# The last two row tiles of a transformer block's output: final products in two column halves, with a hand-written order on two engines

## Chip, cores, metric

One Trainium2 chip, one of its cores. The metric is the device time of the whole kernel in microseconds, the median of several runs. The engines are TensorE (PE, with its weight loads PEld), VectorE (DVE), ScalarE (ACT), GpSimd (POOL) and SyncE (SP, which issues the DMAs). Each works through its own queue in order, and waits for the others on semaphores.

## What is computed

A block of a hybrid encoder: a mixer (pooling and gated linear attention), then a squared-ReLU MLP, then a last RMS norm. The change touches only the end, the second product of the MLP, its residual sum and the last norm:

```python
def rmsnorm(x, g):
    y = xf * lax.rsqrt(jnp.mean(xf * xf, axis=-1, keepdims=True) + EPS)
    return (y * g.astype(jnp.float32)).astype(x.dtype)

def squared_relu_mlp(u, w_ff1, w_ff2):
    hdn = jnp.square(jax.nn.relu(jnp.einsum('bld,df->blf', u, w_ff1)))
    return jnp.einsum('blf,fd->bld', hdn, w_ff2)

# in reference():
        h = h + squared_relu_mlp(rmsnorm(h, norm_ffn[l]), w_ff1[l], w_ff2[l])
    return rmsnorm(h, norm_final)[:, N_META:]
```

The hidden state has 1024 rows (tokens) and 1024 columns, the MLP 4096 hidden channels.

## The kernel before

All products are made of three matmuls each (`mm3`, lines 246 to 248), since both operands are split into a high and a low part. The split of an operand costs one instruction on ACT (L264) and one on DVE (L265).

The second product of the MLP (`ff2`) is a Strassen scheme: seven products `m` = 0 to 6 in place of eight, each of 512 rows by 512 columns over 2048 hidden channels, taken in 16 steps `i` (`NPAIR`). A product works on four row tiles `t` = 0 to 3 of 128 rows, with one PSUM bank of 512 columns for each tile. The table `FF2` says to which quarters of the result `c` each product is added or subtracted; `add` does this on DVE, straight out of PSUM (L1630, L1632). The last product, `m` = 6, goes to one quarter alone: the first 512 columns of row tiles 0 to 3. Rows 4 to 7 are finished earlier.

In that last product the last three steps are held back (`late`). So the four row tiles end one after another instead of all at once: nine matmuls for tile 0, nine for tile 1, nine for tile 2, nine for tile 3. The banks of these four tiles are named b_x, b_x, b_mm and b_ms. Behind each tile its finish follows (`finish_row` with `tail`):

- the addition of the bank to `c` (DVE, L1630);
- the sum of squares of the first 512 columns (ACT Square with its readout, L1605). That of the other 512 columns was made earlier by `top`, which also multiplied these columns by the norm's weight;
- the root: Ln and Exp on ACT (L210, L212), and on DVE the mean (L211) and a Newton step in three instructions (L214, L218, L219);
- the scaling: the right 512 columns on ACT (L1608), the left 512 on DVE (L1609);
- two stores of 256 KB, right and left, both issued by SP (L1611).

Only TensorE's order is written by hand (`manual_schedule` around everything). On ACT, DVE and SP a scheduler sets the order in which the recorded instructions stand.

Of the kernel before, what the change touches and what calls it, by code (L numbers as in the profile page):

```python
# [11 lines left out]
ACT = mybir.ActivationFunctionType  # L12
ALU = mybir.AluOpType
AX = mybir.AxisListType

P = 128
D = 1024
# [3 lines left out]
HALF = 512  # L21
# [4 lines left out]
EPS = 1e-6  # L26
# [4 lines left out]
NPAIR = DFF // P // 2  # L31
# [74 lines left out]
def kernel(  # L106
# [3 lines left out]
    nc = tc.nc  # L110
    x = x[0]
    out = out[0]
# [4 lines left out]
    act, dve, pool, pe = nc.scalar, nc.vector, nc.gpsimd, nc.tensor  # L117
# [20 lines left out]
    def bank(tag):  # L138
        if tag in rota:
            turn_of[tag] = turn_of.get(tag, -1) + 1  # L140
            tag = rota[tag][turn_of[tag] % len(rota[tag])]
        return psp[tag].tile([P, 512], F32, name=f"b_{tag}", tag=tag)
# [20 lines left out]
    gB = left.push("gB", [P, D], F32)  # L163
# [3 lines left out]
    def tiny(n):  # L167
        a = small_at[0]
        small_at[0] += n
        assert small_at[0] <= 128  # L170
        return small[:, a : a + n]

    pscale, bgate, gnorm = tiny(4), tiny(2), tiny(4)
    stat = [tiny(16) for _ in range(4)]
# [22 lines left out]
    def bcast(v):  # L197
        return v[None, :].broadcast_to([P, D])
# [43 lines left out]
    def mm3(ps, n, lhs, rhs, first=True, last=True, more=False):  # L242

        for i in range(n):
            (ah, al), (bh, bl) = lhs(i), rhs(i)
            pe.matmul(ps, ah, bh, start=first and i == 0, stop=False, skip_group_check=more)  # L246
            pe.matmul(ps, ah, bl, start=False, stop=False, skip_group_check=more)  # L247
            pe.matmul(ps, al, bh, start=False, stop=last and i == n - 1, skip_group_check=more)  # L248
# [19 lines left out]
    def ahead(items, n):  # L268

        made = []  # L270
        for x in items:
            made.append(x)
            if len(made) > n:
                yield made.pop(0)
        yield from made
# [125 lines left out]
    S, rings = {}, [W1]  # L401
# [41 lines left out]
    def halves():  # L443
        return [slice(h * HALF, (h + 1) * HALF) for h in range(2)]
# [1138 lines left out]
    def ff2_operands():  # L1583
        for m, i, a in ahead(ff2_raw(), 2):
            q = FF2[m][1]
            w = S["w2"][q[:2]][:, i]
            if len(q) > 2:
                bt = S["bt"][:, i % 2]
                dve.tensor_tensor(bt, w, S["w2"][q[3:]][:, i], ALU.add if q[2] == "+" else ALU.subtract)  # L1589
                w = bt  # L1590
            yield m, i, split(a), split(w)

    def finish_row(t, tail):

        a, (h0, h1) = S["c"][:, t], halves()
        junk = S["w2"]["12"].rearrange("p i c -> p (i c)")[:, (t % 4) * D : (t % 4 + 1) * D]
        if not tail:
            ss = ln_stat[t % 4]
            act.activation(junk, a, ACT.Square, accum_out=ss)
            rs = inv_sqrt(ss, 1, 1.0 / D)  # L1600
            dve.scalar_tensor_tensor(junk, a, rs, gB, ALU.mult, ALU.mult)
            nc.sync.dma_start(out[t * P : (t + 1) * P, :], junk)
            return
        s0, s1 = tails[t]
        act.activation(junk[:, h0], a[:, h0], ACT.Square, accum_out=s0)  # L1605
        dve.tensor_scalar(s1, s1, 1.0 / D, EPS, ALU.mult, ALU.add)
        rs = inv_sqrt(s0, 1, 1.0 / D, s1)
        act.activation(junk[:, h1], a[:, h1], ACT.Copy, scale=rs)  # L1608
        dve.scalar_tensor_tensor(junk[:, h0], a[:, h0], rs, gB[:, h0], ALU.mult, ALU.mult)  # L1609
        for c in (h1, h0):  # L1610
            nc.sync.dma_start(out[t * P : (t + 1) * P, c], junk[:, c])  # L1611

    tails = [(tiny(1), tiny(1)) for _ in range(4)]

    def ff2():
        nc.sync.dma_start(gB, bcast(norm_final))
        h1 = halves()[1]
        b, late, owed = None, [], []

        banks_of = [bank(tag) for tag in ("x", "x", "mm", "ms", "ms", "ms", "ms", "mm")]  # L1620

        def product(t, i, av, bv):
            (ah, al), (bh, bl) = av, bv
            c = slice(t * P, (t + 1) * P)
            mm3(b[t], 1, lambda _: (ah[:, c], al[:, c]), lambda _: (bh, bl), first=i == 0, last=i == NPAIR - 1)

        def add(b, t, r, k, sign):
            a = S["c"][:, 4 * r + t, k * HALF : (k + 1) * HALF]
            if sign > 0:
                dve.tensor_tensor(a, b, a, ALU.add)  # L1630
            else:
                dve.tensor_tensor(a, a, b, ALU.subtract)  # L1632

        def top(t):

            a = S["c"][:, t, h1]
            act.activation(S["w2"]["12"][:, 8 + t], a, ACT.Square, accum_out=tails[t][1])
            dve.tensor_tensor(a, a, gB[:, h1], ALU.mult)

        def leave(m, t):  # L1640

            for at in FF2[m][2]:
                owed.append(lambda b=b[t], at=at: add(b, t, *at))
            if m == 4:
                owed.append(lambda: finish_row(4 + t, False))
            elif m == 5:
                owed.append(lambda: top(t))
            elif m == 6:
                owed.append(lambda: finish_row(t, True))

        for m, i, av, bv in ahead(ff2_operands(), 2):
            if i == 0:
                b = banks_of[m % 2 * 4 : m % 2 * 4 + 4]
            if m == 6 and i >= NPAIR - 3:
                late.append((i, av, bv))
            else:
                for t in range(4):
                    product(t, i, av, bv)
            if owed:
                owed.pop(0)()  # L1660
            if i < NPAIR - 1:
                continue
            for t in range(4):
                for x in late:
                    product(t, *x)
                leave(m, t)
                while m == 6 and owed:
                    owed.pop(0)()

    def ff_layers():  # L1670

        ff_open()
        del rota["mm"]
        run = ff_quarters.run()
        for n in range(4):
            if n in (1, 3):
                turn_tile(ORDER[6 + n // 2])
            next(run)
        ff_room()
        for _ in run:  # L1680
            pass

    for fn in (ff_layers, ff2_open, ff2):
        step(one, fn)
# [47 lines left out]
```

## Time and profile before

| | |
|---|---|
| median of 3 runs | 1234.57 us (1233.56 to 1236.65) |
| the profiled execution | 1233.45 us |
| its span on the core | 1231.7 us |
| TensorE busy | 1204.4 us (98%) |
| DVE busy | 851.8 us (69%) |
| ACT busy | 618.7 us (50%) |
| last matmul of row tile 3 starts | 1223.59 us |
| last stores issued | from 1227.91 us on |

Times in rows are microseconds from the start of the span. A row of the timeline gives the start, the length, the engine, the line, the operation, what is written and read, the shape, and in brackets the idle time before it with what ended it. A row of the chain of waits gives the start, the length, and who held the end at that time. A grouped row ends with the busy time and the mean length in ns. A row of a stretch gives its bounds and length, the busy time of PE, PEld, DVE, ACT and POOL, the granted clock, the DMA share and GB/s.

### The profile page before, as it was taken

What the parts mean: (1) busy time and instruction counts of PE and PEld (TensorE: products, weight loads), DVE (VectorE), ACT (ScalarE), POOL (GpSimd) and SP (SyncE); (2) the same over time, 40 slices, a digit from 0 to 9 for tenths busy, and PEclk for the clock granted to TensorE, in tenths of its full rate; (3) what the DMA queues carried; (4) which work ended last, traced back from release to release, by engine and by line L of the source; (5) the groups of instructions that cost most, each with busy time, mean ns of one, the idle gap of its engine ahead of it and who ended that gap; (6) DMA issues with size and microseconds to landing.
All of it is one profiled execution on the core that took longest, in us unless ns stands there. A gap on an engine that the chain in (4) does not pass through costs nothing.

```text
span 1231.7 us, 18293 instructions
## 1 busy us (share of the span) xinstructions
PE 1204.4 (98%) x6818; PEld 1003.1 (81%) x6818; DVE 851.8 (69%) x1391; ACT 618.7 (50%) x1099; POOL 64.4 (5%) x70
## 2 busy tenths in 40 slices
PE   7999999999999999899999999999999999999997
PEld 7878888978887888688878888888888888888886
DVE  7986675753566676624896676776765887887686
ACT  7667567322446753312654454554554444444554
POOL 2000000001101115300000000000000000000000
PEclk9999999999999999899999999999999999999999
DMA  8043426155112156831244444444469973333532
GB/s 252 2 112 118 121 86 188 52 171 188 36 36 71 60 156 213 294 99 52 99 125 160 156 154 139 163 154 143 163 222 314 345 264 95 98 99 95 164 99 87
DMA packets 141672, 173.84 MB, mean 141 GB/s; under 512 B 9944, under 2 KB 81392, under 8 KB 141584
## 3 DMA queue, kind: packets, MB, share of 16 engines
q1 hardware_dynamic: 141552, 172.62, 43.8%
q8 instruction: 53, 0.87, 0.3%
q14 instruction: 35, 0.29, 0.1%
q0 software_dynamic: 32, 0.07, 0.1%
HBM read 119.17 MB, written 53.48 MB: 140 GB/s over the span
## 4 chain that ended last, share of the span: by engine, by line
PE 85%; DVE 9%; ACT 3%; issue 2%; DMA 1%; POOL 0%; SPq 0%; DVEq 0%; ACTq 0%; POOLq 0%
PE b_mm L246 10%; PE b_mm L247 10%; PE b_mm L248 10%; PE b_ms L247 9%; PE b_ms L246 9%; PE b_ms L248 9%; PE b_x L247 8%; PE b_x L248 8%; PE b_x L246 8%; PE b_sc L1180 1%; PE b_mx L246 1%; PE b_m L1282 1%; PE b_mx L247 1%; PE b_mx L248 1%; DVE t L1093 1%
## 5 line engine op out<-in xcount | busy, mean ns | idle before, releaser
L246 PE MATMUL b_mm<-th,w1h 128*128 128x512 f32 (+1 forms) x312 | 117.6, 377 | 1.4 <-DVE c L794 1.0
L247 PE MATMUL b_mm<-tl,w1h 128*128 128x512 f32 (+1 forms) x312 | 116.0, 372 | 0.6 <-DVE tl L1440 0.6
L248 PE MATMUL b_mm<-th,w1l 128*128 128x512 f32 (+1 forms) x312 | 115.8, 371 | 0.0
L246 PE MATMUL b_x<-th,w1h 128*128 128x512 f32 (+1 forms) x240 | 90.7, 378 | 0.0
L247 PE MATMUL b_x<-tl,w1h 128*128 128x512 f32 (+1 forms) x240 | 90.6, 378 | 0.0
L248 PE MATMUL b_x<-th,w1l 128*128 128x512 f32 (+1 forms) x240 | 90.3, 376 | 0.0
L264 ACT ACTIVATE w1h<-raw 128x512 fp32r<-128x512 f32 x96 | 59.5, 621 | 34.2 <-PE b_x L247 14.2
L265 DVE TENSOR_TENSOR w1l<-raw,w1h 128x512 fp32r<-128x512 f32 x96 | 65.6, 684 | 10.5 <-ACT w1h L264 10.5
L246 PEld LDWEIGHTS b_mm<-th,w1h 128*128 128x128 f32 x312 | 58.6, 188 | 13.1 <-issue 1.4
L264 ACT ACTIVATE w1h<-fs 128x512 fp32r<-128x512 f32 x72 | 45.4, 631 | 45.8 <-PE b_ms L247 31.3
L247 PEld LDWEIGHTS b_mm<-tl,w1h 128*128 128x128 f32 x312 | 58.6, 188 | 10.6 <-DVE tl L1440 0.9
L248 PEld LDWEIGHTS b_mm<-th,w1l 128*128 128x128 f32 x312 | 58.6, 188 | 10.3
L264 ACT ACTIVATE w1h<-bt 128x512 fp32r<-128x512 f32 x44 | 27.8, 632 | 67.9 <-issue 63.6
L265 DVE TENSOR_TENSOR w1l<-fs,w1h 128x512 fp32r<-128x512 f32 x72 | 49.3, 685 | 14.7 <-ACT w1h L264 14.6
L1589 DVE TENSOR_TENSOR bt<-w,w 128x512 f32<-128x512 f32 x80 | 54.6, 683 | 2.1 <-DMA w<-in_w_ff_dram 2.1
L248 PEld LDWEIGHTS b_x<-th,w1l 128*128 128x128 f32 x240 | 45.1, 188 | 8.4
L246 PEld LDWEIGHTS b_x<-th,w1h 128*128 128x128 f32 x240 | 45.0, 188 | 8.5
L247 PEld LDWEIGHTS b_x<-tl,w1h 128*128 128x128 f32 x240 | 45.1, 188 | 8.3
L264 ACT ACTIVATE fxh<-bt 128x512 fp32r<-128x512 f32 x36 | 22.8, 632 | 54.9 <-issue 49.3
L247 PE MATMUL b_ms<-wo,w1h 128*128 128x512 f32 x128 | 49.8, 389 | 0.0
L246 PE MATMUL b_ms<-wo,w1h 128*128 128x512 f32 x128 | 49.8, 389 | 0.0
L248 PE MATMUL b_ms<-wo,w1l 128*128 128x512 f32 x128 | 49.8, 389 | 0.0
(445 smaller groups left out, 3353.9 us busy)
## 6 DMA issues: line engine op xcount, KB each, us to landing
hf_dram<-h SPq DMA_DIRECT2D x112, 256.0 KB, 2.1
raw<-hf_dram SPq DMA_DIRECT2D x112, 256.0 KB, 2.7
w<-in_w_ff_dram SPq DMA_DIRECT2D x64, 256.0 KB, 5.0
raw<-in_w_in_dram SPq DMA_DIRECT2D x24, 512.0 KB, 4.8
raw<-in_w_ff_dram SPq DMA_DIRECT2D x16, 512.0 KB, 4.2
rawx<-in_w_ff_dram SPq DMA_DIRECT2D x16, 512.0 KB, 4.1
xs<-in_x_dram SPq DMA_DIRECT2D x8, 512.0 KB, 5.9
rawx<-in_w_in_dram SPq DMA_DIRECT2D x8, 512.0 KB, 4.3
```

The costliest lines, as they stand in the source:

```text
L246: pe.matmul(ps, ah, bh, start=first and i == 0, stop=False, skip_group_check=more)
L247: pe.matmul(ps, ah, bl, start=False, stop=False, skip_group_check=more)
L248: pe.matmul(ps, al, bh, start=False, stop=last and i == n - 1, skip_group_check=more)
L264: act.activation(hi, a, ACT.Copy)
L265: dve.tensor_tensor(lo, a, f32(hi), ALU.subtract)
L1093: dve.tensor_tensor(gl, b, gl, ALU.mult)
L1180: pe.matmul(b[to, e, j], kk[r, s], qq[r, s], start=True, stop=True, tile_position=(e * CH, u * CH))
L1282: pe.matmul(o[part(u), e, j], scc[part(u), e, j], v[part(u), j, e], start=j == 0, stop=False, tile_position=(u * CH, u * CH), skip_group_c ...
L1589: dve.tensor_tensor(bt, w, S["w2"][q[3:]][:, i], ALU.add if q[2] == "+" else ALU.subtract)
```

## The change

For row tiles 2 and 3 of the last product a new function, `last_rows`, takes the place of `leave` and `finish_row`. It differs in five points.

1. The nine held-back matmuls of a tile become 18 of 256 columns: nine for the first column half of the bank, then nine for the second (`remaining` with `q`). The weights are loaded for each half anew.
2. The addition and the Square of each tile are made in two halves of 256 columns, each with its own accumulator. The first half's sum is added to the other 512 columns' mean in a small instruction on DVE (L1628 of the new kernel).
3. The left scaling on DVE is made in two pieces of 256 columns (L1646).
4. The calls of `last_rows` stand under `manual_schedule` for ACT and DVE.
5. Of the last four stores SP issues three and ACT one: the right half of row tile 3 (L1650).

The accumulation groups of tiles 2 and 3 are marked as ended before the held-back steps (`ends`), and the later matmuls skip the check on groups.

```diff
+    def last_rows(product, b):
+        a = [S["c"][:, t] for t in (2, 3)]
...
+        q = [slice(k * HALF // 2, (k + 1) * HALF // 2) for k in range(2)]
+        h1, rs = halves()[1], [None, None]
+        def add(u, k):
+            dve.tensor_tensor(a[u][:, q[k]], b[2 + u][:, q[k]], a[u][:, q[k]], ALU.add)
+        def square(u, k):
+            act.activation(junk[u][:, q[k]], a[u][:, q[k]], ACT.Square, accum_out=more[u][k])
+        def root(u):
+            (s0, s1), s = more[u], tails[2 + u][1]
+            dve.scalar_tensor_tensor(s, s0, 1.0 / D, s, ALU.mult, ALU.add)
+            rs[u] = s1
...
+            act.activation(y, s1, ACT.Ln, scale=1.0 / D, bias=s)
+            dve.tensor_scalar(v, s1, 1.0 / D, s, ALU.mult, ALU.add)
+            act.activation(y, y, ACT.Exp, scale=-0.5)
+            return v, y, t
+        def newton(u, v, y, t):
+            dve.scalar_tensor_tensor(t, v, y, y, ALU.mult, ALU.mult)
+            dve.tensor_scalar(t, t, -0.5, 1.5, ALU.mult, ALU.add)
+            dve.tensor_tensor(rs[u], y, t, ALU.mult)
+        def right_half(u):
+            act.activation(junk[u][:, h1], a[u][:, h1], ACT.Copy, scale=rs[u])
+        def left_half(u, k):
+            dve.scalar_tensor_tensor(junk[u][:, q[k]], a[u][:, q[k]], rs[u], gB[:, q[k]], ALU.mult, ALU.mult)
+        def store(u, k, eng):
+            c = halves()[k]
+            eng.dma_start(out[(2 + u) * P : (3 + u) * P, c], junk[u][:, c])
+        for u in range(2):
+            s = tails[2 + u][1]
+            dve.tensor_scalar(s, s, 1.0 / D, EPS, ALU.mult, ALU.add)
+        for k in range(2):
+            product(2, q[k])
+            add(0, k)
+            square(0, k)
+        product(3, q[0])
+        z = root(0)
+        add(1, 0)
+        square(1, 0)
+        newton(0, *z)
+        product(3, q[1])
+        add(1, 1)
+        square(1, 1)
+        left_half(0, 0)
+        z = root(1)
+        left_half(0, 1)
+        right_half(0)
+        newton(1, *z)
+        store(0, 0, nc.sync)
+        store(0, 1, nc.sync)
+        right_half(1)
+        for k in range(2):
+            left_half(1, k)
+        store(1, 1, act)
+        store(1, 0, nc.sync)
...
+        def remaining(t, q):
+            for x in late:
+                product(t, *x, q)
...
-            for t in range(4):
-                for x in late:
-                    product(t, *x)
+            if m == 5:
+                ends = NPAIR - 4
+            for t in range(4 if m < 6 else 2):
+                remaining(t, slice(0, HALF))
                 leave(m, t)
...
+        with tc.manual_schedule(engines={mybir.EngineType.Activation, mybir.EngineType.DVE}):
+            last_rows(remaining, b)
```

How the instructions stand. On ACT, from the end of row tile 0's finish into row 1's (`c` is the result, `w_12_7888` the buffer that takes the squares and then the scaled rows, `small` the one-column statistics):

```order
 L210 ACTIVATE small<-small 128x1
-L212 ACTIVATE small<-small 128x1
-L1605 ACTIVATE w_12_7888,small<-c 128x512
+L1624 ACTIVATE w_12_7888,small<-c 128x256
+L212 ACTIVATE small<-small 128x1
 L1608 ACTIVATE w_12_7888<-c,small 128x512
```

The first Square of row tile 2 (L1624) now stands between the Ln (L210) and the Exp (L212) of row tile 1; the whole Square (L1605) stood behind the Exp.

On DVE, from row 0's scaling on, as it stands now:

```order
L1609 TENSOR_SCALAR w_12_7888<-c,small,gB 128x512
L211 TENSOR_SCALAR small<-small 128x1
L1621 TENSOR_TENSOR c<-b_mm,c 128x256
L214 TENSOR_SCALAR small<-small 128x1
L218 TENSOR_SCALAR small<-small 128x1
L219 TENSOR_TENSOR small<-small 128x1
L1609 TENSOR_SCALAR w_12_7888<-c,small,gB 128x512
L1621 TENSOR_TENSOR c<-b_mm,c 128x256
L1628 TENSOR_SCALAR small<-small 128x1
L1633 TENSOR_SCALAR small<-small 128x1
L1621 TENSOR_TENSOR c<-b_ms,c 128x256
```

The first addition of row tile 2 stands where its whole addition stood; the second stands behind row 1's scaling, and row 3's first addition behind two root steps of row 2.

On TensorE, at the change from the first to the second half of row tile 2's bank b_mm (the word in brackets is the engine whose semaphore the matmul waits for):

```order
L246 MATMUL b_mm<-fxh 128x256
L247 MATMUL b_mm<-fxl,fxh 128x256
L248 MATMUL b_mm<-fxh,fxl 128x256
L246 MATMUL b_mm<-w1h 128x256 [waits DVE_49]
L247 MATMUL b_mm<-w1l,w1h 128x256
```

The first matmul of the second half waits for DVE. The bank b_ms of row tile 3 has the same wait at the same place; in the kernel before, no matmul of these two banks' last nine waits for anything.

More of the change, by code (lines that the diff above doesn't have):

```diff
@@ L1611, in finish_row @@
             nc.sync.dma_start(out[t * P : (t + 1) * P, c], junk[:, c])
+    def last_rows(product, b):
+        a = [S["c"][:, t] for t in (2, 3)]
+        junk = [S["w2"]["12"].rearrange("p i c -> p (i c)")[:, t * D : (t + 1) * D] for t in (2, 3)]
+        q = [slice(k * HALF // 2, (k + 1) * HALF // 2) for k in range(2)]
[8 more added lines that the diff above has]
+            rs[u] = s1
+            k = inv_sqrt.k = (inv_sqrt.k + 1) % 2
+            v, y, t = stat[2 * k][:, 0:1], stat[2 * k + 1][:, 0:1], stat[2 * k][:, 8:9]
+            act.activation(y, s1, ACT.Ln, scale=1.0 / D, bias=s)
[40 more added lines that the diff above has]
+        store(1, 0, nc.sync)
@@ L1613 @@
     tails = [(tiny(1), tiny(1)) for _ in range(4)]
+    more = [(tiny(1), tiny(1)) for _ in range(2)]
     def ff2():
@@ L1620, in ff2, with product @@
         banks_of = [bank(tag) for tag in ("x", "x", "mm", "ms", "ms", "ms", "ms", "mm")]
-        def product(t, i, av, bv):
+        def product(t, i, av, bv, q=slice(0, HALF)):
             (ah, al), (bh, bl) = av, bv
             c = slice(t * P, (t + 1) * P)
-            mm3(b[t], 1, lambda _: (ah[:, c], al[:, c]), lambda _: (bh, bl), first=i == 0, last=i == NPAIR - 1)
+            mm3(
+                b[t][:, q], 1, lambda _: (ah[:, c], al[:, c]), lambda _: (bh[:, q], bl[:, q]),
+                first=i == 0, last=i == NPAIR - 1 or i == ends and t > 1, more=t > 1 and i > ends,
+            )
+        ends = NPAIR
+        def remaining(t, q):
+            for x in late:
+                product(t, *x, q)
         def add(b, t, r, k, sign):
```

## The prediction

> **What bounds the kernel now.** I read the page first: the busy shares, then the chain of work that ended last, then that chain and the timeline for the last 15 us.
>
> ```profile
> span 1231.7 us, 18293 instructions
> ...
> PE 1204.4 (98%) x6818; PEld 1003.1 (81%) x6818; DVE 851.8 (69%) x1391; ACT 618.7 (50%) x1099; POOL 64.4 (5%) x70
> ...
> PE 85%; DVE 9%; ACT 3%; issue 2%; DMA 1%; POOL 0%; SPq 0%; DVEq 0%; ACTq 0%; POOLq 0%
> ```
>
> Over the span TensorE is the bound. The change touches only the last stage, so its own limit counts. The chain of waits there:
>
> ```profile
> 1217.63 0.24 PE b_x L248
> 1217.90 0.70 DVE c L1630
> ...
> 1220.80 0.72 ACT w L1605 x2
> ...
> 1224.10 0.62 DVE c L1630
> 1224.74 0.72 ACT w L1605 x2
> 1225.46 0.61 ACT w L1608
> 1226.08 0.19 ACT small L210
> ...
> 1227.16 0.75 DVE w L1609
> ```
>
> The reader is to see that the last TensorE piece on the chain is row tile 0's, at 1217.63. From there the chain runs over DVE and ACT alone. Row 3's matmuls end near 1223.98 (their last one below), yet the last computing instruction ends at 1227.91. So this stage is bound by two in-order queues that carry additions, squares, root steps and scalings, and what matters is what stands ahead of what on them. The rows of the timeline that I build on:
>
> ```profile
> 1219.74 0.39 PE L246 MATMUL b_mm<-w1h 128*128 128x512 f32 x1
> 1219.96 0.39 PE L247 MATMUL b_mm<-w1l,w1h 128*128 128x512 f32 x1
> 1221.05 0.75 DVE L1609 SCALAR_TENSOR_TENSOR w<-c,small,gB 128x512 f32<-128x512 f32 x1
> 1221.72 0.21 DVE L211 TENSOR_SCALAR small<-small 128x1 f32<-128x1 f32 x1
> 1221.98 0.69 DVE L1630 TENSOR_TENSOR c<-b_mm,c 128x512 f32<-128x512 f32 x1
> 1222.35 0.20 ACT L212 ACTIVATE small<-small 128x1 f32<-128x1 f32 x1
> 1223.23 0.75 DVE L1609 SCALAR_TENSOR_TENSOR w<-c,small,gB 128x512 f32<-128x512 f32 x1
> 1223.24 0.19 ACT L1605 ACTIVATION_READ_ACCUMULATOR w<-c 128x1 f32 x1
> 1223.59 0.39 PE L248 MATMUL b_ms<-fxh,fxl 128*128 128x512 f32 x1
> 1224.02 0.69 DVE L1630 TENSOR_TENSOR c<-b_ms,c 128x512 f32<-128x512 f32 x1
> ```
>
> I write (2,0) for row tile 2, first column half of its bank (256 columns), and so on; such work is called half-width.
>
> **The change part by part.** First the prices of half-width work, then each queue. No half-width instruction of these lines exists before; the nearest rows are, first of the timeline, then of the groups:
>
> ```profile
> 330.06 0.28 PE L246 MATMUL b_mx<-vw,th 128*128 128x256 f32 x1
> 330.18 0.28 PE L247 MATMUL b_mx<-vw,th 128*128 128x256 f32 x1
> ```
>
> ```profile
> L499 ACT ACTIVATE v<-b_mm 128x256 f32<-128x256 f32 x15 | 5.6, 374 | 11.8 <-PE b_mm L248 8.5 <-PE b_mx L1125 3.3
> L1226 ACT ACTIVATE mix<-f 128x256 f32<-128x256 f32 x8 | 3.3, 433 | 7.1 <-DVE f L1214 4.1 <-DVE yg L1314 2.0 <-PE b_m L1310 1.0
> L1225 DVE TENSOR_TENSOR mix<-n,ends 128x256 f32<-128x256 f32 x8 | 3.1, 412 | 0.0
> L1275 DVE SCALAR_TENSOR_TENSOR W<-W,ends,b_m 128x128 f32<-128x128 f32 x24 | 8.3, 344 | 0.5
> ```
>
> Matmuls of 256 columns follow each other by 0.12 us (330.06 to 330.18), those of 512 by 0.22 to 0.23. So 36 halves cost 36 x 0.12 = 4.32 us against 18 x 0.227 = 4.09: TensorE loses 0.23 us, if it waits for nothing. A half-width addition: 0.42 us (L1225). A half-width Square: between 0.37 and 0.43, taken 0.42, as L1226 also reads what DVE made. A half-width scaling on DVE lies between 0.344 (128 columns) and 0.75 (512, L1609): by the straight line between them 0.48. On both engines a successor starts some 0.08 us before its predecessor's end (L211 at 1221.72, with L1609 ending at 1221.80). A dependent one on another engine starts about 0.03 us after the end (the addition at 1224.02 ends at 1224.71, the Square starts at 1224.74); after a matmul I take 0.04.
>
> TensorE gains a wait. The order shows the first matmul of the second half of each of these two banks waiting for DVE, and the only DVE work on that bank before it is the first half's addition. The trace has one such case, TensorE held by an addition out of a PSUM bank:
>
> ```profile
> 74.33 0.68 DVE L794 TENSOR_TENSOR c<-b_mm,u3p 128x512 f32<-128x512 f32 x1
> 75.15 0.47 PE L246 MATMUL b_mm<-th,w1h 128*128 128x512 f32 x1 [1.02 <-DVE c L794]
> 75.46 0.40 PE L247 MATMUL b_mm<-tl,w1h 128*128 128x512 f32 x1
> ```
>
> The addition ends at 75.01, the matmul starts at 75.15, its successor 0.31 later instead of 0.23. For nine half-width matmuls behind such a wait that is 0.14 + 0.20 + 7 x 0.12 + 0.28 (the last one's length) = 1.46 us from the end of the addition to the end of the half.
>
> The Trainium skill (PSUM — Partial Sum Buffer, "PSUM bank collisions raise a hardware error") says that two engines must not touch the same bank and partitions at once, even in different columns, and that a semaphore should guard by bank. By that rule the halves of one bank can't overlap at all; the trace of before has no case of two halves in one bank, and for the guard's price only the row at 75.15. By that rule the sum comes to the +2.3 us below; with halves that overlap it would be the +1.4 us of the first rival.
>
> Now the queues, in program order, each instruction starting when its engine is free and its input is there. The same bookkeeping applied to the queues of before ends at 1227.89, where the trace has 1227.91.
>
> Row 2, first half. (2,0) is complete at 1219.74 + 8 x 0.12 + 0.28 = 1220.98. But its addition stands on DVE behind row 0's scaling and row 1's L211, where the whole addition stood: 1221.98 to 1222.40. TensorE waits from 1220.98 to 1222.5.
>
> Row 1's root. ACT now has Square (2,0) between the Ln (L210) and the Exp (L212) of row 1. That Square waits for the addition, runs from 1222.43, and its readout from 1222.77; Exp moves from 1222.35 to 1222.86. DVE's three root steps, queued behind Exp, stand idle, and row 1's scaling moves from 1223.23 to 1223.72: +0.5 us.
>
> Row 2, second half. TensorE is done with it at 1222.40 + 1.46 = 1223.86. Its addition stands behind row 1's scaling: 1224.39 to 1224.81. The Square's readout ends at 1225.36; before, row 2's sum was out at 1223.43. That is 1.9 us late, and nothing has been won by the first half's early start.
>
> Row 3. (3,0) is complete at 1223.86 + 1.08 = 1224.94. Its addition is queued behind the step of row 2's root that needs the readout of 1225.36 (L1633 in the new numbering): 1225.51 to 1225.93. The matmuls of (3,1) wait for it, so that they end at 1225.93 + 1.46 = 1227.39, against 1223.98 before. Addition (3,1): 1227.43 to 1227.85. Before, row 3's addition was over at 1224.71. So +3.14 us up to here.
>
> The finish. Before, from the end of that addition to the end of the last instruction: 1227.91 - 1224.71 = 3.20. Now: Square with its readout until 1228.40, Ln and Exp until 1228.94, three root steps until 1229.56, two half scalings on DVE until 1230.47, and ACT's scaling of row 3 until 1230.31: 2.62. Part of that is the shorter Square (0.21), part that the scaling of row 2 (0.61 in the chain, at 1225.46) no longer stands ahead of row 3's Ln. Won back: 0.58 us. Last computing instruction: 3.14 - 0.58 = +2.56.
>
> The stores. First two rows of the SP queue, the last stores and the program's first load; then the page's row on the stores' landing; then stretches of the span (the last two numbers are the DMA share and GB/s):
>
> ```profile
> 0.74 0.39 SPq L621 DMA_DIRECT2D xs<-in_x_dram  x1
> ...
> 1227.91 0.81 SPq L1611 DMA_DIRECT2D out_dram<-w  x2
> ```
>
> ```profile
> out_dram<-w SPq DMA_DIRECT2D x8, 256.0 KB, 2.1
> ```
>
> ```profile
> 1.50:1.75 0.25, 0.00 (x0) 0.00 (x0) 0.00 (x0) 0.25 (x1) 0.25 (x1) 1.00 0.35 16
> ...
> 1228.75:1230.00 1.25, 0.00 (x0) 0.00 (x0) 0.00 (x0) 0.00 (x0) 0.00 (x0) 0.65 1.01 379
> 1230.25:1231.70 1.45, 0.00 (x0) 0.00 (x0) 0.00 (x0) 0.00 (x0) 0.00 (x0) 0.50 0.00 0
> ```
>
> The two issues of SP began at 1227.91 and, by their 0.81 in all less the length of one, about 1228.33; the execution ended 3.37 after the second. Now ACT issues (3,1) at 1230.34, right behind its own scaling, and SP issues (3,0) at 1230.49, so the last issue is 1230.49 - 1228.33 = 2.16 later: 0.4 us won by the second issuer. With 3.37 behind it the end is 1233.86. On the other hand three stores, (2,1) at 1229.71 and these two, now come within 0.8 us. At 379 GB/s one takes 0.69, so that the data of the last is over at about 1232.55 instead of 1230.15: 2.4 later, which gives 1234.1. I take 1234.0 between them: +2.3 us.
>
> ACT has issued no DMA before this one, and a store from it has no row. Below: nothing, the store is like SP's (2.1 us to landing). Above: SP's own first DMA moved no byte before 1.50, at least 0.76 and at most 1.01 after its issue at 0.74, where the last stores had theirs about 0.8 after the issue; so 0.2 at most. I take nothing, since the row of a first use is that near.
>
> Behind the waiting instructions: SP's queue holds only the other stores at this point, and POOL nothing. All loads of the last product are over. The new accumulators and the early end mark of the accumulation groups add no instruction ahead of 1217.
>
> **Sum.** +0.23 us of TensorE pitch and the waits of (2,1) and (3,1) are inside the +3.14; -0.58 in the finish; -0.4 from the issue by ACT; +0.1 from stores that crowd: +2.3 us. Span 1231.7 + 2.3 = 1234.0, and with the 1.75 us around it (1233.45 less 1231.7) 1235.75 for an execution like the profiled one. That one was 1.1 below the median of the runs, 1234.57; on the median it makes **1236.9 us**.
>
> The bounds of the parts: a half-width scaling of 0.35 instead of 0.48 takes 0.3 us off the end (two of them stand there), one of 0.60 adds 0.3; a half-width Square at 0.37 takes 0.1; a TensorE release like the row's, but with the weight load behind it too, adds 0.2. Together 1236.3 to 1237.5 before the noise of a median, which the runs from 1233.56 to 1236.65 put at some 1 us.
>
> **Rivals.**
>
> First, TensorE isn't held, because the order's wait is met early or is for something else. Then (3,1) is complete at 1224.2, its addition starts behind row 2's root at 1226.54, and the last scaling ends at 1229.58, 0.9 earlier: +1.4 us, **1236.0**. For it: no row shows two halves in one bank. Against it: the order shows the wait, and 75.15 shows that such a wait holds TensorE.
>
> Second, the queues do run by need: additions at once when a half is complete. (3,1) would be complete at 1224.22, added by 1224.68, and with the finish of 2.62 over at 1227.30, 0.6 sooner than before; with the 0.4 of the second issuer -1.0 us, **1233.6**. For it: the chain leaves TensorE 10 us before the end, so there is something to win. Against it: three orders on DVE and ACT (Square ahead of row 1's Exp, row 1's scaling ahead of addition (2,1), row 2's root ahead of addition (3,0)) are fixed, and each costs more than it hides.
>
> Third, on the slower side: ACT's first store lands late, being the first transfer of a queue that has carried nothing. Its place is the very end, where nothing covers it. A store that lands 2.1 to 2.3 after its issue leaves 1.1 to the end (1228.33 + 2.2 to 1231.7). ACT's begins at 1230.34, so it decides from a landing time of 2.6 us on. The nearest other landing times:
>
> ```profile
> raw<-hf_dram SPq DMA_DIRECT2D x112, 256.0 KB, 2.7
> ga_dram<-o SPq DMA_DIRECT2D x16, 256.0 KB, 2.4
> ma_dram<-o SPq DMA_DIRECT2D x16, 256.0 KB, 4.4
> ```
>
> At the 4.4 us of the slowest store of this size the end is 1230.34 + 4.4 + 1.1 = 1235.8, +4.1 us: **1238.7**. For it: no row of an issue by ACT. Against it: the 4.4 stands in a part of the program with much other traffic, and SP's first use was quick.
>
> **How the numbers follow.** Forecast 0.66, first rival 0.12, second 0.04, third 0.18. A change of 0.3% (3.7 us) is about what a measurement of this kernel can tell from no change. The forecast lies 1.4 us inside it, so about one time in eight noise carries it over; the third rival lies 0.4 outside, so it is slower in about three of four of its cases. Slower: 0.66 x 0.12 + 0.18 x 0.75 = 0.22. Faster: only the second rival with luck, or a strayed median: 0.02. Within 0.3%: 0.76. The range takes in the first rival and most of the third with the noise of the median: 1234.5 to 1239.2.
>
> **What would show it.** In the new profile I expect: the 256-column matmuls at a pitch of 0.12; two idle spells of TensorE of 1.5 and about 1 us, each ended by the addition (L1621); row 1's Exp about 0.5 us later than 1222.35; the addition of (2,1) behind row 1's scaling near 1224.4; the last scaling (L1646) ending near 1230.5; the last two stores issued within 0.2 us by ACT and SP; a span near 1234.0. I am wrong if TensorE runs through without idle spells, if the order of the additions is other than printed, or if ACT's store takes much over 2.5 us to land.

## The result, and the profile after

| | before | changed |
|---|---|---|
| median, 22 runs each | 1234.11 us (1232.46 to 1236.65) | 1235.9 us (1234.55 to 1238.74) |
| ratio | | 1.0017, 95% interval [1.0011, 1.0022] |
| the profiled execution | 1233.45 us | 1235.89 us |
| its span | 1231.7 us | 1234.1 us |
| row tile 0's last matmul starts (T0 below) | 1217.47 us | 1217.57 us |
| last computing instruction ends | 1227.91 us, T0 + 10.44 | 1230.40 us, T0 + 12.83 |
| end of the span | T0 + 14.2 | T0 + 16.5 |

The changed kernel is slower by 0.17%, about 2.1 us by the ratio (the two medians lie 1.8 apart). The interval doesn't reach 1, so the loss is clear of the noise, but it is inside the 0.3% called no change. It was predicted at 1236.9 us, with a range from 1234.5 to 1239.2.

The page of the changed kernel, the span, the busy times and the queue that ACT's one store opened (packets, MB, share):

```profile
span 1234.1 us, 18342 instructions
...
PE 1205.4 (98%) x6836; PEld 1004.9 (81%) x6836; DVE 854.1 (69%) x1397; ACT 619.2 (50%) x1103; POOL 64.5 (5%) x70
...
q10 hardware_dynamic: 144, 0.26, 0.1%
```

The busy shares tell nothing: TensorE has 1.0 us more in 1205, and its share is 98% in both. The chain of waits of the changed kernel does (start, length, who held the end):

```profile
1222.24 0.18 ACT small L210
1222.43 0.49 ACT w L1624 x2
1222.92 0.10 ACT small L212
...
1225.56 0.34 DVE c L1621
...
1225.94 0.39 PE b_ms L246
...
1227.16 0.13 PE b_ms L248
...
1227.32 0.43 DVE c L1621
1227.78 0.52 ACT w L1624 x2
```

Two things are new in it. The first Square of row tile 2 (L1624) lies between row 1's Ln and Exp. And TensorE is back on the chain as late as 1227.29, where before it left the chain with row 0's piece at 1217.63. The timeline shows how it got there:

```profile
1219.86 0.28 PE L246 MATMUL b_mm<-w1h 128*128 128x256 f32 x1
1219.97 0.28 PE L247 MATMUL b_mm<-w1l,w1h 128*128 128x256 f32 x1
...
1221.96 0.41 DVE L1621 TENSOR_TENSOR c<-b_mm,c 128x256 f32<-128x256 f32 x1
1222.43 0.39 PE L246 MATMUL b_mm<-w1h 128*128 128x256 f32 x1 [1.33 <-DVE c L1621]
1222.82 0.19 ACT L212 ACTIVATE small<-small 128x1 f32<-128x1 f32 x1
1223.68 0.75 DVE L1609 SCALAR_TENSOR_TENSOR w<-c,small,gB 128x512 f32<-128x512 f32 x1
1224.35 0.42 DVE L1621 TENSOR_TENSOR c<-b_mm,c 128x256 f32<-128x256 f32 x1
...
1225.48 0.41 DVE L1621 TENSOR_TENSOR c<-b_ms,c 128x256 f32<-128x256 f32 x1
...
1225.94 0.39 PE L246 MATMUL b_ms<-w1h 128*128 128x256 f32 x1 [1.10 <-DVE c L1621]
...
1227.32 0.42 DVE L1621 TENSOR_TENSOR c<-b_ms,c 128x256 f32<-128x256 f32 x1 [0.81 <-PE b_ms L248]
...
1228.95 1.80 SPq L1650 DMA_DIRECT2D out_dram<-w  x3
...
1229.52 0.88 DVE L1646 SCALAR_TENSOR_TENSOR w<-c,small,gB 128x256 f32<-128x256 f32 x2
1230.27 0.37 ACTq L1650 DMA_DIRECT2D out_dram<-w  x1
```

Read the brackets first. TensorE stands idle for 1.33 us and again for 1.10 us, each time until the addition of the bank's first half is over. Both additions had been late for reasons of DVE's own queue. Then DVE in its turn waits 0.81 us for TensorE (1227.32). So the two in-order queues hold each other up in a circle.

The stores, in stretches of the changed kernel's span (length, five engines' busy times, clock, DMA share, GB/s):

```profile
1229.60:1230.10 0.50, 0.00 (x0) 0.00 (x0) 0.50 (x2) 0.50 (x1) 0.00 (x0) 0.50 0.63 233
1230.10:1230.60 0.50, 0.00 (x0) 0.00 (x0) 0.29 (x1) 0.14 (x1) 0.00 (x0) 0.50 1.00 377
...
1232.10:1232.60 0.50, 0.00 (x0) 0.00 (x0) 0.00 (x0) 0.00 (x0) 0.00 (x0) 0.50 0.89 340
1232.60:1233.10 0.50, 0.00 (x0) 0.00 (x0) 0.00 (x0) 0.00 (x0) 0.00 (x0) 0.50 0.01 0
```

From 1229.8 to 1232.5 the four stores move without a gap, and the span ends 1.5 us later, as it did before (0 GB/s there from 1230.2 on, end at 1231.7).

### The profile page after: what moved, and what is told of

Its sections match the earlier page's. It is cut to its first block, busy times and chain, and to the rows that moved or that the text cites. A ratio compares the mean times of both kernels' runs of the same rounds, so it can differ in the third digit from the quotient of the medians.

```text
span 1234.1 us, 18342 instructions
## 1 busy us (share of the span) xinstructions
PE 1205.4 (98%) x6836; PEld 1004.9 (81%) x6836; DVE 854.1 (69%) x1397; ACT 619.2 (50%) x1103; POOL 64.5 (5%) x70
## 4 chain that ended last, share of the span: by engine, by line
PE 84%; DVE 9%; ACT 3%; issue 2%; DMA 2%; POOL 0%; SPq 0%; DVEq 0%; ACTq 0%; POOLq 0%
PE b_mm L246 10%; PE b_mm L247 10%; PE b_mm L248 10%; PE b_ms L246 9%; PE b_ms L248 9%; PE b_ms L247 9%; PE b_x L247 8%; PE b_x L246 8%; PE b_x L248 8%; PE b_sc L1180 1%; PE b_mx L246 1%; PE b_m L1282 1%; PE b_mx L248 1%; PE b_mx L247 1%; DVE ut L759 1%
## 5 line engine op out<-in xcount | busy, mean ns | idle before, releaser
L264 ACT ACTIVATE w1h<-raw 128x512 fp32r<-128x512 f32 x96 | 59.5, 620 | 34.5 <-PE b_x L247 14.2
L265 DVE TENSOR_TENSOR w1l<-fs,w1h 128x512 fp32r<-128x512 f32 x72 | 49.4, 687 | 14.5 <-ACT w1h L264 14.4
```

Source lines behind the costliest of these rows:

```text
L264: act.activation(hi, a, ACT.Copy)
L265: dve.tensor_tensor(lo, a, f32(hi), ALU.subtract)
```

## The experiments

What has to be told apart is where the 2.4 us of the end come from: the order on ACT and DVE, the wait between the halves of one bank, the halves as such, or the stores. In all experiments the end of the program (row tiles 0 to 3 of the last product) is written as one list of instructions for each engine. In the diffs P is a row's nine or 18 held-back matmuls, A the addition, Q the Square, L and E the Ln and Exp, V the mean, N M O the Newton steps, S the sum of the halves, R the right scaling (ACT), F the left (DVE), s a store by SP, a by ACT. The first digit is the row tile, the second the column half. In the rows of these runs the addition is L1646, the Square L1649, the sum of the halves L1652, Ln L1656, the mean L1658, Exp L1660, the Newton step L1662 to L1666, the right scaling L1668, the left L1670, the stores L1673.

Single executions differ by up to 2.3 us in what lies ahead of the end, though hardly an instruction differs there (T0 lies from 1216.28 to 1218.58 in the ten profiles). So the parts of the end are measured inside each profile, from T0, and each comes from one execution. Two pairs of kernels whose computing instructions stand in the same order show how well that repeats: 12.83 and 12.82 (changed and sp_store), 10.15 and 10.15 (the two whole_root3). A span is given to 0.1 us, and so are the stretches to its end.

| run | last computing instruction ends, T0 + | span ends, T0 + | median, us | ratio to before |
|---|---|---|---|---|
| before | 10.44 | 14.2 | 1233.97 and 1234.26, 33 runs each | 1 |
| changed | 12.83 | 16.5 | 1235.9 | 1.0017 [1.0011, 1.0022] |
| exp_first | 12.47 | 16.2 | 1236.36 | 1.0018 [1.0009, 1.0027] |
| own_banks | 11.93 | 15.6 | 1235.12 | 1.0008 [0.9999, 1.0017] |
| sp_store | 12.82 | 16.6 | 1236.32 | 1.0016 [1.0008, 1.0025] |
| pe_halves | 10.71 | 14.5 | 1233.87 | 0.9998 [0.9989, 1.0006] |
| need_guard | 11.63 | 15.4 | 1234.48 | 1.0007 [0.9998, 1.0016] |
| need_banks | 10.87 | 14.6 | 1234.24 | 1.0001 [0.9992, 1.001] |
| whole_root3 | 10.15 | 13.9 | 1234.06 | 1.0 [0.9992, 1.0009] |
| whole_root3_act | 10.15 | 14.1 | 1234.18 | 1.0 [0.9991, 1.0009] |

### One instruction of the order: row 1's Exp ahead of the Square

```diff
 ACT, from the changed kernel
-L1 Q20 E1 R1
+L1 E1 Q20 R1
```

> The changed kernel with one instruction moved on ACT: row 1's Exp ahead of the first Square of row 2, instead of behind it. Order theory (the loss is what stands ahead of what on ACT and DVE, plus TensorE's wait for the first half's addition): row 1's scaling, the addition of (2,1), that of (3,0) and everything behind them move 0.5 us forward; span 1233.6 against 1234.1. Rival 'halves' (the narrow matmuls and the added instructions cost it): no difference, 1234.1. Rival 'ACT store' (the store issued by ACT costs it): 1234.1.

The Exp of row 1 and TensorE's second wait in this run (the first wait is as long as in the changed kernel, 1.34):

```profile
1223.43 0.39 PE L246 MATMUL b_mm<-w1h 128*128 128x256 f32 x1 [1.34 <-DVE c L1646]
1223.46 0.20 ACT L1660 ACTIVATE small<-small 128x1 f32<-128x1 f32 x1
...
1226.60 0.39 PE L246 MATMUL b_ms<-w1h 128*128 128x256 f32 x1 [0.76 <-DVE c L1646]
```

The Exp starts at T0 + 4.88 where the changed kernel has 5.25, 0.37 sooner, and the last computing instruction comes 0.36 sooner. The shift runs through to the end undiminished, and most of it shows in TensorE's second wait (0.76 for 1.10). So this one instruction costs 0.36 us, somewhat less than the half microsecond expected. The profiled span (1234.8) is longer than the changed kernel's all the same, since T0 came 1.0 us later in this execution. In the median the gain can't be seen either, as the two ratios' intervals cover each other.

### The wait between halves taken away: a bank of its own for each half

```diff
+def own_bank(t):    # when the held-back steps are still to come
+    at = c[:, t, 256:512]
+    dve.tensor_tensor(at, b[t][:, 256:512], at, ALU.add)
+    second[t] = banks_of[4 + t]
...
-product of the second half into b[t][:, 256:512]
+product of the second half into second[t][:, 256:512]
```

What stands in the second half when the held-back steps begin is added to the result early, and these steps then sum up in another bank. The order on ACT and DVE stays that of the changed kernel.

> The changed kernel, but the held-back matmuls of the second halves go to two PSUM banks of their own, so that TensorE waits for no addition; what these columns had before is added to the result earlier, in DVE's idle time at 1215. Orders on ACT and DVE as in the changed kernel. Order theory: TensorE runs through, (3,1) is complete near 1224.3 instead of 1227.3, and the addition of (3,1) then waits only for DVE: 0.9 us off the end, span 1233.2. Rival 'halves': nothing gained, two more additions, 1234.1 or a little more. Rival 'ACT store': 1234.1.

The chain of waits of this run, at the place where the changed kernel has the matmuls of b_ms:

```profile
1226.16 0.34 DVE c L1646
...
1226.95 0.16 DVE small L1666
1227.12 0.35 DVE c L1646
1227.48 0.52 ACT w L1649 x2
```

TensorE is off the chain. The second addition of row 3 (1227.12) waits for nothing but its turn behind row 2's Newton steps. No matmul of these banks waits any more, and 0.90 us come back at the last computing instruction, as much as the prediction's first rival had put on a TensorE that isn't held. That settles that TensorE's waits are real and cost this much, and that they are not the whole: 1.5 us of the 2.4 stay. The wait goes with the shared bank and not with shared data, since the halves are other columns of it. It is a semaphore that the program sets (`[waits DVE_49]` in the order of the change). The Trainium skill (PSUM — Partial Sum Buffer, "PSUM bank collisions raise a hardware error") asks for just such a guard by bank. The runs show what the guard costs, 1.33 and 1.10 us of waiting with one bank and none with two, and not whether it is needed: what happens without it was not tried.

### The store by ACT undone

```diff
-s20 s21 a31 s30
+s20 s21 s31 s30
```

> The changed kernel with all stores issued by SP. If the end is set by the last issue, as in the forecast's first sum, it comes 0.3 to 0.4 us later: span 1234.4 to 1234.5. If it is set by the rate at which three crowded stores move their data, nothing changes: 1234.1. Rival 'ACT store': the loss goes, span 1232 to 1233.

```profile
1229.57 0.88 DVE L1670 SCALAR_TENSOR_TENSOR w<-c,small,gB 128x256 f32<-128x256 f32 x2
```

This row of the timeline puts the last computing instruction at 1230.45, T0 + 12.82, and the span ends at 1234.2, 3.75 later. The changed kernel has 3.70 from its last computing instruction to the end. The second issuer wins nothing that can be measured. The reason stands in the stretches above: a store of 256 KB takes 0.69 us at 379 GB/s, an issue only 0.4, so while one store moves, the issue of the next one is hidden anyway. In sp_store too the data move without a gap: the DMA share is 0.95 or more in every stretch of 0.5 us from 1230.10 to 1232.60. The Trainium skill (DMA: Bandwidth & Descriptors, "Issuing engines are not separate DMA queues") says that issuing from several engines saves only the time of the issue itself; here not even that is saved.

Nor did ACT's store land late. In the changed kernel it took 2.2 us (the row of the DMA issues: size and us from issue to landing), and 2.2 to 2.8 us in the six kernels that have it:

```profile
out_dram<-w ACTq DMA_DIRECT2D x1, 256.0 KB, 2.2
```

### The halves on TensorE alone

```diff
-P20, A20, Q20, P21, A21, Q21 (halves everywhere, changed kernel)
+P20, P21, A2, Q2             (halves on TensorE, the rest as before)
```

> The kernel before, with only the held-back matmuls of row tiles 2 and 3 in two column halves (36 of 256 columns instead of 18 of 512); additions, squares, scalings and stores whole and in the old order, so that no half waits for DVE. Order theory: TensorE ends 0.2 us later, DVE takes up most of it since it was busy then: span 1231.7 to 1231.9. Rival 'halves': most of the loss is here, span 1233 or more. Rival 'ACT store': 1231.7.

In this run the additions and all else stand as in the kernel before. The price shows at the addition of row 2, which now waits for TensorE, and at row 3's last matmul and addition:

```profile
1222.27 0.69 DVE L1646 TENSOR_TENSOR c<-b_mm,c 128x512 f32<-128x512 f32 x1 [0.18 <-PE b_mm L248]
...
1224.11 0.28 PE L248 MATMUL b_ms<-fxh,fxl 128*128 128x256 f32 x1
...
1224.42 0.69 DVE L1646 TENSOR_TENSOR c<-b_ms,c 128x512 f32<-128x512 f32 x1
```

T0 is 1217.62 here. TensorE ends at T0 + 6.77, 0.26 us later than before (1223.98, T0 + 6.51), and the last computing instruction ends 0.27 us later. Twice as many matmuls of half the width cost about what their pitch says (0.23). That DVE would take up most of it was expected and didn't come true: from T0 the span is 0.25 longer, where at most 0.2 was expected. In the kernel before, row 3's addition (1224.02) starts 0.04 us after its last matmul ends (1223.98), so TensorE was as near to binding there as DVE's queue, though the chain of waits names only DVE. The narrow matmuls alone are a small part of the 2.39.

### The order by need, with one bank and with two

```diff
 DVE, from the changed kernel
-F0 V1 A20 N1 M1 O1 F1 A21 S2 V2 A30 N2 M2 O2 A31
+A20 F0 V1 N1 M1 O1 A21 F1 S2 A30 V2 N2 M2 O2 A31      (need_guard)
+A20 F0 V1 A21 N1 M1 O1 A30 F1 S2 V2 A31 N2 M2 O2      (need_banks)
 ACT
-L1 Q20 E1 R1 Q21 L2 E2 Q30 Q31
+L1 E1 Q20 R1 Q21 L2 E2 Q30 Q31                        (need_guard)
+L1 E1 Q20 Q21 R1 Q30 L2 E2 Q31                        (need_banks)
```

> Halves and their shared banks stay as in the changed kernel; only the order on ACT and DVE moves: each half is added where it is complete (the addition of (2,0) ahead of row 0's scaling, of (2,1) and (3,0) ahead of what waits for ACT), and row 1's Exp stands ahead of the Square of (2,0). I count from the start of row 0's last matmul to the end of the span: 14.2 us before, 16.5 changed, 16.2 with the Exp alone moved. Order and guard theory (part of the loss is the order, part the wait of TensorE for the half's addition, and the two feed each other): 15.3 us, so about 1.2 of the lost 2.3 comes back, TensorE still waits for additions but less than 1.3 us each time, median about 1.1 us above before. Rival, the order is the whole loss: 14.2 or less. Rival, the guard is the whole loss once it is there: 16 or more.

> As the run with the order by need, and each half has its own bank, so that TensorE waits for no addition in the tail. Two more additions stand ahead of the tail on DVE, where it is idle. Order and guard theory: what is left of the loss goes, the stretch from row 0's last matmul to the end is 14.2 to 14.4 us like before (14.2): halves by need are no quicker than whole rows, since more half-width instructions with their fixed cost stand on the two queues, and the stores' data leave at the same rate; median within 0.5 us of before. Rival (halves by need start the chain earlier and win): 13.6 or less. Rival (something else of the change costs): 15 or more.

With the shared bank and the better order, TensorE's waits are still there, but shorter:

```profile
1222.38 0.39 PE L246 MATMUL b_mm<-w1h 128*128 128x256 f32 x1 [0.52 <-DVE c L1646]
...
1225.52 0.39 PE L246 MATMUL b_ms<-w1h 128*128 128x256 f32 x1 [0.73 <-DVE c L1646]
```

The last computing instruction ends at T0 + 11.63, 1.20 us sooner than in the changed kernel. That is what the order theory asked for (15.3 to the end of the span), and both rivals' bounds (14.2 or less, 16 or more) are missed: it measured 15.4.

With own banks as well it is 10.87. The order alone gave 1.20 and the banks alone 0.90; both together give 1.96, nearly the sum. But need_banks also has another order than need_guard (the last two lines of each part of the diff), so the 0.76 between these two can't be put down to the banks alone. Of the changed kernel's 2.39 this leaves 0.43. The end of the span came at T0 + 14.6, not at the 14.2 to 14.4 that I had expected. The median is that of before, as expected; for need_guard it is 0.9 us above before by the ratio, where 1.1 had been expected. Where the 0.43 lies is seen in need_banks' timeline, beside the Ln of row 3 in the kernel before:

```profile
1225.98 0.28 ACT L210 ACTIVATE small<-small 128x1 f32<-128x1 f32 x1
```

and in need_banks:

```profile
1222.74 0.28 PE L248 MATMUL b_mm<-fxh,fxl 128*128 128x256 f32 x1
...
1222.99 0.18 ACT L1649 ACTIVATION_READ_ACCUMULATOR w<-c 128x1 f32 x1
...
1224.14 0.19 ACT L1649 ACTIVATION_READ_ACCUMULATOR w<-c 128x1 f32 x1
...
1224.82 0.15 DVE L1652 SCALAR_TENSOR_TENSOR small<-small 128x1 f32<-128x1 f32 x1
...
1225.07 0.29 ACT L1656 ACTIVATE small<-small 128x1 f32<-128x1 f32 x1 [0.74 <-DVE small L1652]
...
1226.27 0.88 DVE L1670 SCALAR_TENSOR_TENSOR w<-c,small,gB 128x256 f32<-128x256 f32 x2
```

T0 is 1216.28 here. TensorE's last matmul ends at T0 + 6.74, 0.23 later than before (T0 + 6.51). The squares of row 3's second half are summed at T0 + 8.05 (1224.14 + 0.19). Before, the whole row's were at T0 + 8.00 (1225.28 + 0.19), so up to here the early start of the first halves has won nothing. Then row 3's Ln waits 0.74 us for the sum of the two halves (L1652), an instruction that whole rows don't need. The Ln starts at T0 + 8.79, before at 8.51 (1225.98): 0.28. From the Ln to the last scaling it takes 1.20 (1225.07 to 1226.27), before 1.18 (1225.98 to 1227.16). And the two half scalings take 0.88 where one whole one took 0.75: 0.13.

The largest of these, the wait for L1652, is again a matter of order. The sum of row 3's first half was read out by 1223.17 (1222.99 + 0.18), but L1652 stands on DVE behind row 2's Newton steps and a scaling of row 2 and starts at 1224.82. If it stood ahead of them, the Ln could start near T0 + 8.07, and with the same 1.20 and 0.88 behind it the last computing instruction would end near T0 + 10.15. That is an estimate, and no run has this order. So the orders that were tried lose, but it isn't shown that halves must. By the estimate they would come out level with whole rows after the swap that follows here, which end at T0 + 10.15 as well.

### Whole rows, with one swap on ACT

The prediction found part of the gain in the finish by taking row 2's scaling from ahead of row 3's Ln. That part can be had without halves, with SP's store or with ACT's:

```diff
 ACT, from the kernel before
-Q3 R2 L3 E3 R3
+Q3 L3 E3 R2 R3
 stores (whole_root3_act only)
-s31 s30
+a31 s30
```

> No halves, one issuer: before's kernel with one swap on ACT, row 3's Ln and Exp ahead of the scaling of row 2's right half, so that DVE's root steps for row 3 run beside that scaling. Theory (the finish is bound by what stands ahead of row 3's Ln on ACT): the Ln moves up by the 0.61 us of the scaling, the last computing instruction by some 0.4, and the stretch from row 0's last matmul to the end from 14.2 to about 13.8. Rival (the stores' data set the end): the scaling of row 2 is now late, its store joins the last two and three stores at 0.69 us each follow without a gap: 14.2 or more. In the whole time either is under 0.05%, so the stretch decides and not the median.

> As the run with row 3's root ahead of row 2's scaling, and the store of row 3's right half is issued by ACT instead of SP. Rate theory (what ends the span is the last store's data, whoever issues it): within 0.15 us of that run's stretch. Issue theory (a second issuer saves the first's 0.4 us): 0.4 us shorter.

The timeline of the first of the two:

```profile
1226.14 0.75 DVE L1670 SCALAR_TENSOR_TENSOR w<-c,small,gB 128x512 f32<-128x512 f32 x1
...
1226.71 0.20 ACT L1660 ACTIVATE small<-small 128x1 f32<-128x1 f32 x1
1226.81 0.21 DVE L1658 TENSOR_SCALAR small<-small 128x1 f32<-128x1 f32 x1
...
1227.12 0.22 DVE L1662 SCALAR_TENSOR_TENSOR small<-small 128x1 f32<-128x1 f32 x1
...
1227.76 0.75 DVE L1670 SCALAR_TENSOR_TENSOR w<-c,small,gB 128x512 f32<-128x512 f32 x1
```

The last computing instruction and the span both end 0.3 us sooner than before, not the full 0.4: the mean (L1658) is ready to run when the Square's readout is out, but stands behind row 2's left scaling on DVE until 1226.81, and the first Newton step starts 0.21 after the Exp is over. The rival of the stores, 14.2 or more, falls. The median is that of before (1.0, from 0.9992 to 1.0009): 0.3 us in 1234 is too little to be told.

ACT's store is no gain here either. Its stretches and those of its sister with SP alone, each with the two last stores in it, first ACT's:

```profile
1228.80:1229.30 0.50, 0.00 (x0) 0.00 (x0) 0.00 (x0) 0.00 (x0) 0.00 (x0) 0.50 0.52 193
...
1230.30:1230.80 0.50, 0.00 (x0) 0.00 (x0) 0.00 (x0) 0.00 (x0) 0.00 (x0) 0.50 0.67 242
```

and SP's:

```profile
1228.80:1229.30 0.50, 0.00 (x0) 0.00 (x0) 0.00 (x0) 0.00 (x0) 0.00 (x0) 1.00 0.67 250
...
1230.30:1230.80 0.50, 0.00 (x0) 0.00 (x0) 0.00 (x0) 0.00 (x0) 0.00 (x0) 0.50 0.84 324
```

By the share of the last stretch the data end at about 1230.63 and 1230.72, that is T0 + 12.40 with ACT's issue and T0 + 12.36 without. From T0 the two spans end at 14.1 and 13.9, so a second issuer doesn't take 0.4 us off here either. Two stores of 0.69 us need about 1.4 us from the first one's data on, whoever issues the second.

## Why the prediction was right, and where its sum was not

Points that held, in the order of its steps:

- TensorE's pitch: 0.11 to 0.12 us in the row of 1219.97, as taken. pe_halves puts the whole price at 0.27; 0.23 was forecast.
- TensorE held by the addition of the bank's first half: both waits are there, 1.33 and 1.10 us where about 1.5 and 1 were forecast. own_banks shows that they go with the shared bank.
- The order on the two queues: the addition of (2,0) at 1221.96 (forecast 1221.98), row 1's Exp at 1222.82 (1222.86), the addition of (2,1) at 1224.35 (1224.39), that of (3,0) at 1225.48 (1225.51), that of (3,1) at 1227.32 (1227.43), the end of the last scaling at 1230.40 (1230.47). Row by row the bookkeeping of the queues was within 0.11 us. Part of that is luck: T0 came 0.1 us later in this execution, and counted from T0 these rows come 0.12 to 0.21 us sooner than forecast. The swap of Exp and Square alone was worth 0.36 us, and the whole order 1.20.
- The first rival (TensorE isn't held) fell with the brackets of the timeline, the second (the queues run by need) with the order. need_guard and need_banks show that the second would not have come to a gain in the orders tried: they end at 11.63 and 10.87, before at 10.44. Whether it would in an order without the wait for L1652 stays open.
- The third rival, a late first store of ACT, fell too: it landed 2.2 us after its issue, where this rival needed more than 2.6. SP's last issue begins at about 1230.4 and ACT's at 1230.27, and the end is no later than sp_store's, where ACT issues nothing.

Points that were off:

- The step "0.4 us won by the second issuer" was wrong. Between the last computing instruction and the end lie 3.79 us before, 3.70 in the changed kernel, 3.75 with SP alone. The prediction counted both an issue time that is hidden and, with its +0.1, too little of the stores that crowd. Net it forecast -0.3 for this part, and -0.1 came.
- The addition of (2,0) was put where the whole addition had stood, T0 + 4.51. It starts at T0 + 4.39: the whole one had waited for the last of its nine matmuls (1219.74 + 8 x 0.227 + 0.39 = 1221.95), the half doesn't. And TensorE is released 0.06 us after the end of the addition (1222.37 to 1222.43), not 0.14, so that the half behind the wait took 1.43 us from addition to addition (1225.89 to 1227.32) in place of 1.50. These two are 0.12 and 0.07; the finish took 0.04 more than forecast.
- The errors have opposite signs: the computing part is 2.39 us longer from T0 instead of 2.56, the stretch from there to the end 0.1 shorter instead of 0.3. The span grew by 2.4 in the two profiled executions, of which 0.1 is T0's, against a forecast of 2.3. That the forecast of the sum is better than its parts is luck.
- The absolute number was 1.0 us too high. About half of that is the starting point: the median of before was 1234.57 in the three runs that were known and 1234.11 in 22. The rest is the 2.3 forecast against the 1.8 between the two medians, which the noise of medians may explain: in the profiled pair the span grew by 2.4.
- The stage was taken as bound by the two queues alone, since the chain leaves TensorE at 1217.63. pe_halves shows TensorE level with them at row 3: ending 0.26 later it moves the end by 0.27. The forecast didn't suffer, as its sum goes over the waits of TensorE.

The shares of the loss, at the last computing instruction: taking the order of need_guard gives 1.20 back, taking the shared bank away gives 0.90, and both, with a further change of order, 1.96 of 2.39. Of the 0.43 left, 0.28 is the Ln's wait for the sum of the halves, which hangs on the order too, and 0.13 is the second half scaling. And the 0.43 is net of a gain: all runs with the changed kernel's finish have row 2's right scaling behind row 3's Exp, and with whole rows that swap is worth 0.29. Against whole_root3, which has it as well, need_banks is 0.72 behind.

## What to carry to other kernels

Splitting the last tiles lets work start earlier only if every in-order queue takes the early piece up at once: before splitting, write down for each piece what stands ahead of it on its engine, and whether its bank holds up the engine that fills it. That goes for the smallest instructions too: one sum of a single column, placed behind a scaling, held the last Ln up for 0.74 us here. Splitting the producer within one bank made it wait for the reader, which a bank for each piece avoided. And a second engine to issue stores was worth nothing here, where a store's data take longer than its issue (0.69 against 0.4 us).

## What the runs showed of the hardware that was not expected

- From the end of the last computing instruction to the end of the span it took 3.7 to 3.9 us in all ten kernels, whether the last row came in one scaling or two, with two stores or four moving in a row, and with one issuing engine or two. The last 1.5 to 1.7 us of it follow the last byte in the records (1232.55 to 1234.1 in the changed kernel, 1230.2 to 1231.7 before, 1230.63 to 1232.3 in whole_root3_act).
- A queue that had carried nothing (q10, ACT's) shows no clear cost at its first use. With it this part is 0.05 us shorter in one pair (changed 3.70, sp_store 3.75) and 0.13 longer in the other (whole_root3_act 3.92, whole_root3 3.79), with spans given to 0.1 us.
